# Loading the first group of rows in pieces of 6, 31 and 28 in place of 6, 28 and 31

## The chip, the core and the metric

The kernel runs on one core of a Trainium2 chip. The metric is the device time of one execution in microseconds. Three engines matter here: VectorE (DVE in the profile), which multiplies, ScalarE (ACT), which computes two sigmoids and a few rows, and SyncE (SP), which issues most DMAs. The 16 DMA engines of the core move the data; each of the two queues that are used here (q1, filled by SP, and q10, filled by ACT) is served in order, and the 16 engines share the packets of each transfer.

## What is computed

For 16,384 rows (tokens) of 512 float32 numbers, the two largest of 8 router logits are turned into two weights, and each row is written twice, once times each weight, the smaller first.

```python
    probs = probs / np.sum(probs, axis=-1, keepdims=True)
    topk_indices = np.argsort(probs, axis=-1)[..., -k:]
    topk_probs = np.take_along_axis(probs, topk_indices, axis=-1)
    topk_probs = topk_probs / np.sum(topk_probs, axis=-1, keepdims=True)
    x_expanded = x[:, :, np.newaxis, :].repeat(k, axis=2)
    return (x_expanded * topk_probs[..., np.newaxis]).astype(np.float32)
```

33.6 MB of rows and 0.5 MB of logits are read, 67.1 MB are written. With two weights left, the quotient of exponentials is a sigmoid of the difference of the two logits.

## The kernel before

Each of the 128 partitions holds 128 rows. They are worked in two groups, of 65 and 63 rows per partition (`GROUPS`); "a row" below means one row on each partition, 256 KB in all. `xs` holds the x rows of a group (65 rows of 2 KB per partition), `osp` has room for 18 output rows of 4 KB. `WA` holds the two weights of every row.

For a group, the loop over `LOADS[g]` (lines 121 to 146) issues the loads, each a run of consecutive rows. Behind the first load of group 1 (6 rows) SP issues the two loads of logits, which land in `osp`, and `top2_weights` (lines 15 to 38) computes all weights on VectorE and ScalarE. Then the loop over `STORES[g]` (lines 148 to 177) makes the outputs. Each entry is (first row, number of rows, place, position there): the multiply at line 164 writes the rows twice, times the weights, into `osp` or, for "xs", in place over rows of `xs` that are no longer needed, and line 176 issues the store, from ACT for the very first, from SP for all others. SP issues in the order of the program, and a DMA that has to wait holds up those behind it.

Group 1 has five stores: 3 rows through `osp` 0 to 2, 15 rows (3 to 17) through `osp` 3 to 17, 16 rows (18 to 33) in place, 15 rows (34 to 48) through `osp` 0 to 14, and 16 rows (49 to 64) in place. The fourth overwrites buffers of the first and the second. Its multiply is therefore cut in two (`FREE`, line 152): 3 rows (34 to 36), which need only the first store to have landed, and 12, which need the second. The order in which the instructions stand on VectorE is made by the scheduler of the language, the DMAs keep the order of the program.

Group 2 begins by loading over `xs`: a load of 4 rows from ACT, held back by a small operation (line 128) until the last store but one of group 1 has landed, then 28 and 31 rows from SP. Its four stores follow the same pattern, with a cut of 2 and 13 rows.

Of the kernel before, what the change touches and what calls it, by code (L numbers as in the profile page):

```python
# [1 line left out]

# [4 lines left out]

F32 = mybir.dt.float32
ALU = mybir.AluOpType
ACTF = mybir.ActivationFunctionType  # L10
P = 128


def top2_weights(nc, WA, dlt, room, logits, E):

    tt = nc.vector.tensor_tensor
    hi, lo, n = None, None, E  # L20
    while n > 1:
        n //= 2
        if hi is None:
            a, b = logits[:, :, 0:n], logits[:, :, n : 2 * n]
            nhi, nlo = room(n), b
            tt(nhi, a, b, op=ALU.max)  # L26
            tt(nlo, a, b, op=ALU.min)  # L27
        else:
            a, b = hi[:, :, 0:n], hi[:, :, n : 2 * n]
            nhi, nlo, tmp = room(n), room(n), room(n)  # L30
            tt(tmp, lo[:, :, 0:n], lo[:, :, n : 2 * n], op=ALU.max)  # L31
            tt(nlo, a, b, op=ALU.min)  # L32
            tt(nlo, nlo, tmp, op=ALU.max)  # L33
            tt(nhi, a, b, op=ALU.max)  # L34
        hi, lo = nhi, nlo
    tt(dlt, hi[:, :, 0], lo[:, :, 0], op=ALU.subtract)  # L36
    nc.scalar.activation(WA[:, :, 0], dlt, ACTF.Sigmoid, scale=-1.0)  # L37
    nc.scalar.activation(WA[:, :, 1], dlt, ACTF.Sigmoid, scale=1.0)  # L38

GROUPS = [65, 63]

LOADS = [[6, 28, 31], [4, 28, 31]]
BASE = [0, 1]

STORES = [
    [(0, 3, "osp", 0), (3, 15, "osp", 3), (18, 16, "xs", 0), (34, 15, "osp", 0), (49, 16, "xs", 33)],
    [(0, 16, "osp", 2), (16, 16, "xs", 0), (32, 15, "osp", 0), (47, 16, "xs", 32)],
]  # L50

L = 18

FREE = [3, 2]

ACT_ROWS = 2


@with_exitstack
def kernel(  # L60
    ctx: ExitStack,
    tc: tile.TileContext,
    x: bass.AP,
    router_logits: bass.AP,
    k: bass.AP,
    out: bass.AP,
):
    nc = tc.nc
    B, S, D = x.shape
    E = router_logits.shape[-1]  # L70
    N = B * S
    assert int(k) == 2 and E == 8 and N == P * sum(GROUPS)
    M = N // P

    x_v, o_v, rl_v = [], [], []
    t0 = 0
    for n in GROUPS:
        t1 = t0 + P * n
        x_v.append(
            x.rearrange("b s d -> (b s) d")[t0:t1].rearrange("(p m) d -> p m d", p=P)  # L80
        )
        o_v.append(
            out.rearrange("b s k d -> (b s) k d")[t0:t1].rearrange(
                "(p m) k d -> p m k d", p=P
            )
        )
        rl_v.append(
            router_logits.rearrange("b s e -> (b s) e")[t0:t1].rearrange(
                "(p m) e -> p m e", p=P
            )  # L90
        )
        t0 = t1

    wpool = ctx.enter_context(tc.tile_pool(name="wpool", bufs=1))
    xs = wpool.tile([P, max(GROUPS), D], F32)
    osp = wpool.tile([P, L, 2, D], F32)
    WA = wpool.tile([P, M, 2], F32)
    dlt = wpool.tile([P, M], F32)


    flat = osp.rearrange("p l k d -> p (l k d)")
    taken = [0]

    def room(n):
        o = taken[0]
        taken[0] += M * n
        return flat[:, o : o + M * n].rearrange("p (m n) -> p m n", n=n)

    logits = room(E)

    def place(where, at, n):

        if where == "osp":
            return osp[:, at : at + n]
        return xs[:, at : at + 2 * n, :].rearrange("p (r k) d -> p r k d", k=2)

    m0 = 0
    stores = []
    for g, G in enumerate(GROUPS):
        x0, r = BASE[g], 0  # L120
        for n in LOADS[g]:

            late = g == 1 and r == 0
            if late:


                rows = xs[:, x0 : x0 + 2, :]
                pause = nc.scalar.activation(rows, rows, ACTF.Copy)  # L128
                tc.add_manual_dep(
                    pause.ins,  # L130
                    stores[-2].ins.name,
                    mybir.DependencyInfo(
                        mybir.DependencyClass.Sync, mybir.DependencyReason.DATA
                    ),
                    reason="begin when the store ahead of the last has landed",
                )
                tc.keep_in_program_order(pause)
            queue = nc.scalar if late else nc.sync
            load = queue.dma_start(xs[:, x0 + r : x0 + r + n, :], x_v[g][:, r : r + n, :])  # L139
            tc.keep_in_program_order(load)  # L140
            r += n
            if g == 0 and r == 6:
                n0 = GROUPS[0]
                tc.keep_in_program_order(nc.sync.dma_start(logits[:, :n0], rl_v[0]))  # L144
                tc.keep_in_program_order(nc.sync.dma_start(logits[:, n0:], rl_v[1]))  # L145
                top2_weights(nc, WA, dlt, room, logits, E)
        assert r == G
        for r, n, where, at in STORES[g]:
            og = place(where, at, n)

            again = where == "osp" and at == 0 and r > 0
            cuts = [0, FREE[g], n] if again else [0, n]
            if g == 1 and r == 0:
                cuts = [0, n - ACT_ROWS]
                for j in range(n - ACT_ROWS, n):
                    for k2 in range(2):
                        nc.scalar.activation(  # L157
                            og[:, j, k2, :],
                            xs[:, x0 + r + j, :],
                            ACTF.Copy,  # L160
                            scale=WA[:, m0 + r + j, k2 : k2 + 1],
                        )
            for a, b in zip(cuts, cuts[1:]):
                nc.vector.tensor_tensor(  # L164
                    og[:, a:b],
                    xs[:, x0 + r + a : x0 + r + b, :]
                    .unsqueeze(2)
                    .to_broadcast([P, b - a, 2, D]),
                    WA[:, m0 + r + a : m0 + r + b, :]
                    .unsqueeze(3)  # L170
                    .to_broadcast([P, b - a, 2, D]),
                    op=ALU.mult,
                )

            queue = nc.scalar if g == r == 0 else nc.sync
            stores.append(queue.dma_start(o_v[g][:, r : r + n], og))  # L176
            tc.keep_in_program_order(stores[-1])
        m0 += G


# [1 line left out]
_INS = ['x', 'router_logits', 'k']  # L182
_OUTS = [((16, 1024, 2, 512), 'float32')]

_NUMBERS = {'k': 2}


# [26 lines left out]
```

## Time and profile before

| | us |
|---|---|
| three runs: median (lowest to highest) | 239.54 (239.52 to 239.55) |
| the profiled execution, its own time | 239.64 |
| its span, first to last instruction | 237.9 |
| VectorE busy | 139.8 |
| ScalarE busy | 5.4 |
| TensorE, GpSimd | nothing that counts |

Line numbers in the profile are those of the listing above. A row of the timeline has the start, the duration, the engine, the line, the operation, the tile written and the tile read, their shapes in elements per partition (1,024 of the output to a row: 3072 is three rows, 15360 fifteen, 16384 sixteen), and in brackets the idle time before it and what ended it. "SPq" and "ACTq" are DMA issues. A row of the windows has the stretch, its length, the busy time of VectorE, ScalarE and GpSimd with their instructions, the clock, the busy share of the DMA engines and GB/s; DMA packets count in the window in which they start. Rows of DMA issues give the KB of each and the us from issue to landing.

### The profile page before, as it was taken

What the parts mean: (1) busy time and instruction counts of PE and PEld (TensorE: products, weight loads), DVE (VectorE), ACT (ScalarE), POOL (GpSimd) and SP (SyncE); (2) the same over time, 40 slices, a digit from 0 to 9 for tenths busy, and PEclk for the clock granted to TensorE, in tenths of its full rate; (3) what the DMA queues carried; (4) which work ended last, traced back from release to release, by engine and by line L of the source; (5) the groups of instructions that cost most, each with busy time, mean ns of one, the idle gap of its engine ahead of it and who ended that gap; (6) DMA issues with size and microseconds to landing.
All of it is one profiled execution on the core that took longest, in us unless ns stands there. A gap on an engine that the chain in (4) does not pass through costs nothing.

```text
span 237.9 us, 111 instructions
## 1 busy us (share of the span) xinstructions
DVE 139.8 (59%) x22; ACT 5.4 (2%) x8; POOL 0.2 (0%) x4
## 2 busy tenths in 40 slices
DVE  0650499999689999200000009999976999950000
ACT  2000000000000000010000003000000000000000
POOL 0000000000000000000000000000000000000000
DMA  7989998989998989989998999898998989989894
GB/s 266 550 357 481 441 408 375 486 351 496 397 463 353 529 362 465 496 353 415 555 397 350 444 479 470 384 507 364 485 397 386 496 353 507 465 362 518 353 529 176
DMA packets 2448, 101.19 MB, mean 425 GB/s; under 512 B 272, under 2 KB 400, under 8 KB 528
## 3 DMA queue, kind: packets, MB, share of 16 engines
q1 hardware_dynamic: 2160, 98.57, 96.2%
q10 hardware_dynamic: 288, 2.62, 2.6%
HBM read 34.08 MB, written 67.11 MB: 425 GB/s over the span
## 4 chain that ended last, share of the span: by engine, by line
DMA 49%; DVE 39%; SPq 1%; issue 0%; DVEq 0%
DMA xs<-in_x_dram 29%; DVE osp L164 25%; DMA out_dram<-osp 19%; DVE xs L164 14%; SPq L144 0%; SPq L145 0%; SPq L139 0%; SPq L176 0%; DVEq L164 0%
## 5 line engine op out<-in xcount | busy, mean ns | idle before, releaser
L164 DVE TENSOR_TENSOR osp<-xs,WA 128x3072 f32<-128x3072 f32 (+5 forms) x7 | 67.2, 9604 | 63.5 <-DMA xs<-in_x_dram 56.9
L164 DVE TENSOR_TENSOR xs<-xs,WA 128x16384 f32<-128x16384 f32 x4 | 68.9, 17225 | 0.2
L26 DVE TENSOR_TENSOR osp<-osp 128x512 f32<-128x512 f32 x1 | 0.7, 691 | 8.1 <-DMA osp<-in_router_logits_dram 8.1
L157 ACT ACTIVATE osp<-xs,WA 128x512 f32<-128x512 f32 x4 | 2.6, 709 | 37.6 <-DMA xs<-in_x_dram 37.6
L128 ACT ACTIVATE xs<-xs 128x1024 f32<-128x1024 f32 x1 | 1.1, 1056 | 91.1 <-DMA out_dram<-osp 91.1
L37 ACT ACT_TABLE_LOAD x1 | 1.3, 1283 | 0.7 <-PEq L195 0.7
L27 DVE TENSOR_TENSOR osp<-osp 128x512 f32<-128x512 f32 x1 | 0.7, 691 | 0.0
L32 DVE TENSOR_TENSOR osp<-osp 128x256 f32<-128x256 f32 (+1 forms) x2 | 0.7, 352 | 0.0
L34 DVE TENSOR_TENSOR osp<-osp 128x256 f32<-128x256 f32 (+1 forms) x2 | 0.7, 351 | 0.0
L33 DVE TENSOR_TENSOR osp<-osp 128x256 f32<-128x256 f32 (+1 forms) x2 | 0.7, 351 | 0.0
L31 DVE TENSOR_TENSOR osp<-osp 128x256 f32<-128x256 f32 (+1 forms) x2 | 0.7, 350 | 0.0
L37 ACT ACTIVATE WA<-dlt 128x128 f32<-128x128 f32 x1 | 0.3, 315 | 10.0 <-DVE dlt L36 10.0
L36 DVE TENSOR_TENSOR dlt<-osp 128x128 f32<-128x128 f32 x1 | 0.3, 291 | 0.0
L38 ACT ACTIVATE WA<-dlt 128x128 f32<-128x128 f32 x1 | 0.3, 298 | 0.0
L195 POOL MEMSET const-uint8-127<- 128x1 uint8 x1 | 0.1, 102 | 0.0
L195 POOL MEMSET const-bfloat16-1.0<- 128x1 bf16 x1 | 0.1, 101 | 0.0
L195 POOL MEMSET const-float32-0.0<- 128x1 f32 x1 | 0.1, 98 | 0.2 <-issue 0.2
L195 POOL MEMSET const-float32-1.0<- 128x1 f32 x1 | 0.1, 98 | 0.0
## 6 DMA issues: line engine op xcount, KB each, us to landing
out_dram<-osp SPq DMA_DIRECT2D x3, 7680.0 KB, 23.3
xs<-in_x_dram SPq DMA_DIRECT2D x2, 7936.0 KB, 40.7
xs<-in_x_dram SPq DMA_DIRECT2D x2, 7168.0 KB, 35.1
xs<-in_x_dram SPq DMA_DIRECT2D x1, 1536.0 KB, 5.9
out_dram<-osp ACTq DMA_DIRECT2D x1, 1536.0 KB, 24.8
xs<-in_x_dram ACTq DMA_DIRECT2D x1, 1024.0 KB, 24.8
osp<-in_router_logits_dram SPq DMA_DIRECT2D x1, 260.0 KB, 6.2
osp<-in_router_logits_dram SPq DMA_DIRECT2D x1, 252.0 KB, 6.3
```

The costliest lines, as they stand in the source:

```text
L26: tt(nhi, a, b, op=ALU.max)
L27: tt(nlo, a, b, op=ALU.min)
L31: tt(tmp, lo[:, :, 0:n], lo[:, :, n : 2 * n], op=ALU.max)
L32: tt(nlo, a, b, op=ALU.min)
L33: tt(nlo, nlo, tmp, op=ALU.max)
L34: tt(nhi, a, b, op=ALU.max)
L36: tt(dlt, hi[:, :, 0], lo[:, :, 0], op=ALU.subtract)
L37: nc.scalar.activation(WA[:, :, 0], dlt, ACTF.Sigmoid, scale=-1.0)
L128: pause = nc.scalar.activation(rows, rows, ACTF.Copy)
L157: nc.scalar.activation(og[:, j, k2, :], xs[:, x0 + r + j, :], ACTF.Copy, scale=WA[:, m0 + r + j, k2 : k2 + 1],)
L164: nc.vector.tensor_tensor(og[:, a:b], xs[:, x0 + r + a : x0 + r + b, :] .unsqueeze(2) .to_broadcast([P, b - a, 2, D]), WA[:, m0 + r + a : ...
L195: nc = _bacc.Bacc("TRN2", target_bir_lowering=False, num_devices=1)
```

## The change

Only the sizes of the first group's second and third load are exchanged:

```diff
-LOADS = [[6, 28, 31], [4, 28, 31]]
+LOADS = [[6, 31, 28], [4, 28, 31]]
```

Rows 34 to 36, which came with the third load, now come with the second. The stores, their rows and their buffers are as they were. In the compiled kernel SP issues 128x15872 elements before 128x14336, and on VectorE one instruction stands elsewhere and the wait for the third load has gone to another (`-` before, `+` after; the elements are those per partition, the waits are those for DMAs):

```diff
 L164 TensorTensor osp<-xs,WA 128x15360    waits for: second load
+L164 TensorTensor osp<-xs,WA 128x3072    waits for: first store
 L164 TensorTensor xs<-xs,WA 128x16384
-L164 TensorTensor osp<-xs,WA 128x3072    waits for: third load, first store
-L164 TensorTensor osp<-xs,WA 128x12288    waits for: second store
+L164 TensorTensor osp<-xs,WA 128x12288    waits for: second store, third load
```

ScalarE, GpSimd and TensorE have the same instructions in the same order.

## The prediction

> **What bounds the kernel now.** I read the page first, then windows that cover the whole execution, then the timeline of the first group, and last, narrow windows at the places where one transfer follows another.
>
> ```profile
> span 237.9 us, 111 instructions
> ...
> DMA packets 2448, 101.19 MB, mean 425 GB/s; under 512 B 272, under 2 KB 400, under 8 KB 528
> ...
> DMA 49%; DVE 39%; SPq 1%; issue 0%; DVEq 0%
> ```
> ```profile
> 42.00:82.00 40.00, 37.29 (x5) 0.00 (x0) 0.00 (x0) 1.00 1.00 431
> 82.00:122.00 40.00, 14.37 (x1) 1.06 (x1) 0.00 (x0) 1.00 1.04 449
> 122.00:162.00 40.00, 19.56 (x2) 2.56 (x4) 0.00 (x0) 1.00 0.98 423
> 162.00:202.00 40.00, 36.59 (x4) 0.00 (x0) 0.00 (x0) 1.00 1.02 442
> 202.00:236.00 34.00, 9.62 (x1) 0.00 (x0) 0.00 (x0) 1.00 0.97 420
> ```
>
> In a windows row the last two columns are the mean busy share of the 16 DMA engines and GB/s; a packet is put down whole to the window in which it starts. From 42 to 236 us, in five equal steps but for the last, the share stays between 0.97 and 1.04: there is no stretch in which the DMA engines lack work, and 101.19 MB must pass through them. VectorE is on 39% of the chain of waits, but only because each of its waits ends with a transfer that is itself in a full queue. So the kernel is bound by the DMA engines, and a microsecond in which they idle is a microsecond of the end. The question for any edit here is not whether VectorE waits longer, but whether the DMA queue runs dry.
>
> ```profile
> 15.91 0.38 ACTq L176 DMA_DIRECT2D out_dram<-osp  x1
> 26.82 16.16 DVE L164 TENSOR_TENSOR osp<-xs,WA 128x15360 f32<-128x15360 f32 x1 [10.94 <-DMA xs<-in_x_dram]
> 43.00 0.35 SPq L176 DMA_DIRECT2D out_dram<-osp  x1
> 43.01 17.22 DVE L164 TENSOR_TENSOR xs<-xs,WA 128x16384 f32<-128x16384 f32 x1
> 60.15 3.35 DVE L164 TENSOR_TENSOR osp<-xs,WA 128x3072 f32<-128x3072 f32 x1
> 60.26 0.34 SPq L176 DMA_DIRECT2D out_dram<-xs  x1
> 66.15 12.96 DVE L164 TENSOR_TENSOR osp<-xs,WA 128x12288 f32<-128x12288 f32 x1 [2.64 <-DMA out_dram<-osp]
> 79.13 0.33 SPq L176 DMA_DIRECT2D out_dram<-osp  x1
> ```
>
> I number the stores of group 1 as the list STORES has them, 1 to 5. Store 2 (15 rows) is issued at 43.00, store 3 (16 rows, in place in `xs`) at 60.26, store 4 at 79.13. The three-row multiply at 60.15 prepares the beginning of store 4 and runs after the large multiply whose end lets store 3 go.
>
> ```profile
> 44.60:44.70 0.10, 0.10 (x1) 0.00 (x0) 0.00 (x0) 1.00 1.61 635
> 47.10:47.15 0.05, 0.05 (x1) 0.00 (x0) 0.00 (x0) 1.00 2.85 1229
> 65.20:65.25 0.05, 0.00 (x0) 0.00 (x0) 0.00 (x0) 1.00 0.00 0
> 65.25:65.30 0.05, 0.00 (x0) 0.00 (x0) 0.00 (x0) 1.00 6.07 2622
> 65.70:65.80 0.10, 0.00 (x0) 0.00 (x0) 0.00 (x0) 1.00 1.52 655
> 65.80:67.60 1.80, 1.45 (x1) 0.00 (x0) 0.00 (x0) 1.00 0.00 0
> ```
>
> The last packets of the third load begin from 44.6 us on, the first packets of store 2 at 47.1, those of store 3 between 65.25 and 65.8. Store 2's 7.86 MB (15 rows of 4 KB on 128 partitions) from 47.1 to 65.25 is 433 GB/s, full rate. So store 2 waited 4.1 us in the queue before its first packet, and store 3 five (65.25 - 60.26). These two leads are the reserve that the change spends.
>
> **The change, part by part.** Bytes, instructions and DMAs keep their number: 6, 31 and 28 rows are issued in place of 6, 28 and 31, on the same queue, and no wait is new in kind. Two things move.
>
> First, the second load is 3 rows longer. They are 3 x 128 x 2048 B = 0.786 MB, at the rate of 434 GB/s that the next row shows 1.81 us.
>
> ```profile
> DMA packets 256, 13.01 MB, mean 434 GB/s; under 512 B 48, under 2 KB 48, under 8 KB 48
> ```
> ```profile
> 15.60:16.20 0.60, 0.28 (x1) 0.00 (x0) 0.00 (x0) 1.00 3.53 1529
> 17.70:18.30 0.60, 0.00 (x0) 0.00 (x0) 0.00 (x0) 1.00 3.78 1529
> 23.05:23.60 0.55, 0.00 (x0) 0.00 (x0) 0.00 (x0) 1.00 3.99 1460
> 25.50:26.50 1.00, 0.00 (x0) 0.00 (x0) 0.00 (x0) 1.00 1.08 457
> ```
>
> (The 434 GB/s are the stretch from 40 to 70 us.) Packets of the second load start 2.1 us apart, one per engine. Its last ones start at 23.05 to 23.6 and the next packets, small ones of store 1, from 25.5 on: about 0.4 us more than 2.1. If that excess does not come again, the load lands only 1.4 us later; if one more of store 1's packets (12,288 B at 434/16 = 27.1 GB/s, 0.45 us) slips in ahead of its end, 2.3 later. I take 1.8, the bytes alone: the 15-row multiply begins at 28.63 (28.2 to 29.1) and ends 16.16 later, and store 2 is issued at 44.81 in place of 43.00. The third load ends when it did, at 47.1 to 47.65, since the bytes of all loads together are the same. So store 2 still has 2.3 us of lead; its nearest relation is the first store of group 2:
>
> ```profile
> 157.51 0.34 SPq L176 DMA_DIRECT2D out_dram<-osp  x1
> ```
> ```profile
> 158.40:160.00 1.60, 1.60 (x1) 0.00 (x0) 0.00 (x0) 1.00 0.00 0
> 160.00:160.10 0.10, 0.10 (x1) 0.00 (x0) 0.00 (x0) 1.00 1.52 655
> ```
>
> It was issued 2.5 us ahead of its first packet and the load before it was at full rate to the end. I cost this part at nothing; the cover is the last packets of the third load, and where it fails by 0.2 to 0.3 us the loss isn't added to what follows, since the lanes would then be busy that much longer with store 2.
>
> Second, rows 34 to 36, which the three-row multiply reads, now come with the second load and not with the third. In the order of the compiled kernel that multiply has moved ahead of the 16-row one on VectorE. It no longer waits for the third load (the 12-row multiply does, which runs long after that has landed); it still waits for store 1, whose buffer it overwrites. That store landed at 40.7:
>
> ```profile
> out_dram<-osp ACTq DMA_DIRECT2D x1, 1536.0 KB, 24.8
> ```
>
> 15.91 + 24.8. Even 2 us later this is before 44.8, so the wait costs nothing. But the 3.35 us of the multiply now stand ahead of the 16-row one and of store 3, which was not so before:
>
> - 28.63 + 16.16 + 3.35 - 0.08 (neighbours overlap: 43.01 + 17.22 is 60.23, the next began at 60.15) + 17.22 = 65.3, and store 3 is issued some 0.03 later, at 65.33 (64.9 to 65.8).
>
> That is 5.1 us later than 60.26, and the reserve was 5.0. SP has nothing else queued between stores 2 and 3, and ACT's queue is empty, so when store 2's last packets end at 65.25 to 65.8 the engines have nothing. What is lost is the time from the issue of a DMA into an empty queue to its running at full rate. No store of before shows this; the first load does:
>
> ```profile
> 0.73 0.37 SPq L139 DMA_DIRECT2D xs<-in_x_dram  x1
> xs<-in_x_dram SPq DMA_DIRECT2D x1, 1536.0 KB, 5.9
> ```
> ```profile
> 1.60:1.70 0.10, 0.00 (x0) 0.10 (x1) 0.00 (x0) 1.00 0.00 0
> 1.70:1.80 0.10, 0.00 (x0) 0.10 (x1) 0.00 (x0) 1.00 2.93 737
> ```
>
> First packet 1.0 us after the issue. Of its 5.9 us to landing, 1.57 MB take 3.6 at 434 GB/s and the end about 0.4 (the engines turned from store 2 to store 3 by 65.75, and VectorE was released by store 2's landing at 66.15). That leaves 1.9 us for start and filling. From above, the store at 157.51 bounds it at 2.5, as no gap was seen there. Between 1.0 and 2.5 I take 1.5, the middle of the two readings of the first load, which is the only DMA on an empty queue.
>
> - Sum: 65.33 + 1.5 - 65.5 (the middle of the starts of store 3 before) = +1.3 us. Bounds: 64.9 + 1.0 - 65.5 = +0.4 and 65.8 + 2.5 - 65.5 = +2.8.
>
> The Trainium skill ("DMA: Bandwidth & Descriptors", section "Latency and other measured facts") gives about 600 ns to the first byte for DMAs issued as these are; by that the sum would be +0.4. The same page ("Anatomy of one DMA") has about 2.0 us of fixed cost per DMA, most of it the receipt at the end; by that, +1.8. The first load's 1.0 lies above the one figure, and its 1.9 by the other.
>
> Where the delay goes: store 4's multiply needs store 2 landed (66.15) and VectorE free (65.3), so it begins at 66.15 as before, and store 4 is still issued at 79.13, now with 1.3 us more reserve. Everything behind store 3 in the queue moves by 1.3 us, and the loads of group 2 with it. There each stage waits for a landing and none for the clock, and the windows above show no idle stretch that could absorb it. So it reaches the end whole.
>
> The profiled execution took 239.64 us (span 237.9 and 1.7 around it), 0.10 above the median of 239.54. 239.64 + 1.3 = 240.9; from the median 240.85, which I forecast.
>
> **Rivals.**
>
> *No loss, or a small gain.* The last packets of the third load took from 44.6 to 47.1, about 2.5 us, where 63,488 B at 27.1 GB/s are 2.34. In group 2, where the store is issued only as the last load packets begin, no such excess is seen:
>
> ```profile
> 157.70:157.75 0.05, 0.05 (x1) 0.00 (x0) 0.00 (x0) 1.00 2.93 1270
> ```
>
> 157.72 to 160.08 is 2.36. If an early store in the queue slows the last load packets, the change removes 0.15 us: 239.4. For it to show, store 3's issue would have to be covered: the three-row multiply would have to stay behind the 16-row one. Then store 3 goes at 28.63 + 16.16 + 17.22 = 62.0, over 3 us ahead of need, and 239.4 to 239.5 stands. Against it speaks the compiled order. It would also do if a store on an empty queue began within 0.2 us, and the first load's 1.0 speaks against that. Chance 0.09 for no difference, 0.03 for a gain above 0.5 us, which I can derive from no row.
>
> *A larger loss at the same place.* Start-up costs the full 2.5 us and load 2 lands at 29.1: +2.8, 242.3. It decides once the first packet of store 3 begins after 68. Chance 0.08. Only the overlap of the store at 157.51 leaves it open.
>
> *Store 2 is the one that starves.* If 2.3 us of lead are too few, there is a gap at 47.4 too. With 2.5 needed it is 0.2; store 2 then frees the engines 0.2 later and store 3's gap shrinks by as much. The end stays at 240.85; above 2.5 the group 2 row excludes it. So it has no time of its own, only another place, chance 0.05 and counted with the forecast.
>
> **How the numbers follow.** The main case (store 3 starves the queue, +0.4 to +2.0) has 0.80 and the larger loss 0.08; no change 0.09, gain 0.03. A measurement of this kernel tells about 0.2%, 0.5 us, from no change; of the main case the lowest corner, +0.4, falls under that, some 0.03. So faster 0.03, within 0.2% 0.12, slower 0.85. The range of 240.0 to 241.9 goes from +0.5 to +2.4: it leaves out the gain, most of no change and the top of the larger loss, under 2 in 10.
>
> **What would show it.** Right: in the changed profile the 15-row multiply begins near 28.6, a 3.35 us multiply stands between it and the 16-row one, store 3 is issued near 65.3, windows between 65.8 and 66.3 have packets still missing that should have started, and store 4 is still issued near 79.1, while the first large multiply of group 2, in the row below, begins 1.3 later. Wrong: packets of store 3 that begin by 65.8 as before; a gap at 47 instead; a three-row multiply that waits beyond 44.8; or a shift at 66 that is gone by 142.
>
> ```profile
> 142.35 15.09 DVE L164 TENSOR_TENSOR osp<-xs,WA 128x14336 f32<-128x14336 f32 x1 [45.98 <-DMA xs<-in_x_dram]
> ```

## The result and the profile after

| | median us | lowest to highest | runs |
|---|---|---|---|
| before | 239.55 | 239.52 to 239.67 | 5 |
| changed | 241.65 | 241.54 to 241.78 | 5 |

The ratio is 1.0087, with a 95% interval of 1.0072 to 1.0102: 2.1 us slower, on the forecast side and inside the range, 0.8 us above the forecast time. The profiled execution took 241.65.

The page and the windows of the changed kernel:

```profile
span 239.9 us, 112 instructions
...
DMA packets 2448, 101.19 MB, mean 422 GB/s; under 512 B 272, under 2 KB 400, under 8 KB 528
```
```profile
42.00:82.00 40.00, 39.17 (x5) 0.00 (x0) 0.00 (x0) 1.00 0.98 426
82.00:122.00 40.00, 14.33 (x1) 1.06 (x1) 0.00 (x0) 1.00 0.98 419
122.00:162.00 40.00, 17.83 (x2) 2.56 (x4) 0.00 (x0) 1.00 1.00 426
```

The same packets and bytes as before, in a span 2.0 us longer. Two microseconds are lost in 240, so a window of 40 us shows them only in its last digits, and an edge that takes in one packet more or less (0.97 to 1.04 before) moves as much. The timeline places them:

```profile
44.94 0.35 SPq L176 DMA_DIRECT2D out_dram<-osp  x1
48.09 17.22 DVE L164 TENSOR_TENSOR xs<-xs,WA 128x16384 f32<-128x16384 f32 x1
65.34 0.34 SPq L176 DMA_DIRECT2D out_dram<-xs  x1
66.11 12.96 DVE L164 TENSOR_TENSOR osp<-xs,WA 128x12288 f32<-128x12288 f32 x1 [0.80 <-DMA out_dram<-osp]
79.09 0.33 SPq L176 DMA_DIRECT2D out_dram<-osp  x1
...
105.48 0.34 ACTq L139 DMA_DIRECT2D xs<-in_x_dram  x1
...
144.08 15.09 DVE L164 TENSOR_TENSOR osp<-xs,WA 128x14336 f32<-128x14336 f32 x1 [47.75 <-DMA xs<-in_x_dram]
...
182.28 14.03 DVE L164 TENSOR_TENSOR osp<-xs,WA 128x13312 f32<-128x13312 f32 x1 [3.60 <-DMA out_dram<-osp]
```

and, for the two of these that were not shown of before:

```profile
104.70 0.34 ACTq L139 DMA_DIRECT2D xs<-in_x_dram  x1
...
180.33 14.03 DVE L164 TENSOR_TENSOR osp<-xs,WA 128x13312 f32<-128x13312 f32 x1 [3.37 <-DMA out_dram<-osp]
```

Each of these rows hangs on a landing, so its shift is what the DMA queue has lost by then: 0 at 66 (66.11 against 66.15), 0.78 at 105, 1.73 at 144, 1.95 at 182. The loss has four places. Windows of the changed kernel at each of them (packets count where they start):

```profile
65.34:66.10 0.76, 0.00 (x0) 0.00 (x0) 0.00 (x0) 1.00 0.01 0
66.10:66.20 0.10, 0.09 (x1) 0.00 (x0) 0.00 (x0) 1.00 7.67 3277
66.20:66.35 0.15, 0.15 (x1) 0.00 (x0) 0.00 (x0) 1.00 11.25 4806
108.60:108.85 0.25, 0.00 (x0) 0.00 (x0) 0.00 (x0) 1.00 10.79 4194
122.45:122.70 0.25, 0.00 (x0) 0.00 (x0) 0.00 (x0) 1.00 11.56 4194
159.40:159.95 0.55, 0.55 (x1) 0.00 (x0) 0.00 (x0) 1.00 4.86 1847
```

and of the kernel before at the last three:

```profile
107.50:108.05 0.55, 0.00 (x0) 0.00 (x0) 0.00 (x0) 1.00 4.40 1907
...
121.00:121.65 0.65, 0.00 (x0) 0.00 (x0) 0.00 (x0) 1.00 4.02 1739
...
157.70:158.30 0.60, 0.60 (x1) 0.00 (x0) 0.00 (x0) 1.00 3.90 1693
```

First, store 3 is issued at 65.34 and no data packet starts for 0.76 us; then five start by 66.20 and the other eleven by 66.35 (3277 GB/s over 0.10 us and 4806 over 0.15, in packets of 65,536 bytes). That is the gap.

The other three are no gaps: the next transfers were long in the queue. The packets took longer. As a packet counts whole where it starts, share times length is the mean time of an engine's packets that start there, and each of the three windows holds one packet per engine.

| window | where | mean time of a packet, changed | before |
|---|---|---|---|
| 108.60 | packets of store 5 just ahead of the first ones of the four-row load | 2.70 | 2.42 |
| 122.45 | turn from store 5 to group 2's loads | 2.89 | 2.42 |
| 159.40 | turn from group 2's loads to its first store | 2.67 | 2.34 |

(The row of before at 121 also holds ten packets of 8 KB of the four-row load, 0.19 us of its 2.61.) That is 0.28, 0.47 and 0.33 us. With the 0.76 of the gap the means add up to 1.84 of the 1.95; a transfer has landed only when its slowest engine is done, so means can fall short.

### The profile page after: what moved, and what is told of

It reads as the page before. It is cut to its first block, busy times and chain, and to the rows that moved or that the text cites. A ratio compares the mean times of both kernels' runs of the same rounds, so it can differ in the third digit from the quotient of the medians.

```text
span 239.9 us, 112 instructions
## 1 busy us (share of the span) xinstructions
DVE 139.7 (58%) x22; ACT 5.4 (2%) x8; POOL 0.2 (0%) x4
## 4 chain that ended last, share of the span: by engine, by line
DMA 49%; DVE 39%; SPq 1%; issue 0%; DVEq 0%
DMA xs<-in_x_dram 31%; DVE osp L164 24%; DMA out_dram<-osp 18%; DVE xs L164 14%; SPq L144 0%; SPq L145 0%; SPq L139 0%; SPq L176 0%; DVEq L164 0%
```

## The experiments

Times are medians, each beside the kernel before on the same chip in the same session (239.60 to 239.70). Single executions of the kernel before reach 240.83 and 240.98 in two of these sessions, so one high time in a run is not a loss of that run.

### Is the gap the whole cause?

Theory 1 was that the emptied queue causes the 0.75 us and the slow packets behind it too. Run 1 puts the three-row multiply back behind the 16-row one:

```diff
+                made = nc.vector.tensor_tensor(
...
+                if g == 0 and r > 3:
+                    tc.keep_in_program_order(made)
```

> Loads of 6, 31 and 28 rows as in the changed kernel, but the three-row multiply stands behind the 16-row one again, as before the change. Theory 1 (the gap ahead of store 3 is the cause of the whole 2.1 us: 0.75 us directly and some 1.2 us in slower packets behind it): store 3 is issued near 62.0, its first packets begin at 65.2 to 65.4 with no gap, no slow packets in group 2, and the time is 239.3 to 239.6. Rival (the late store 2, or the sizes of the loads, are what slow the later packets): no gap at 65 either, but the packets near 109, 122 and 159 us are still slow, and the time is 240.4 to 240.8.

241.73 (241.46 to 241.98), 2.06 above before. The gap is gone, the loss isn't:

```profile
62.24 0.34 SPq L178 DMA_DIRECT2D out_dram<-xs  x1
```
```profile
65.20:65.38 0.18, 0.18 (x1) 0.00 (x0) 0.00 (x0) 1.00 5.93 2563
65.38:65.90 0.52, 0.10 (x1) 0.00 (x0) 0.00 (x0) 1.00 2.62 1132
...
124.46:124.80 0.34, 0.00 (x0) 0.00 (x0) 0.00 (x0) 1.00 2.33 795
...
160.10:160.80 0.70, 0.70 (x1) 0.00 (x0) 0.00 (x0) 1.00 2.38 1030
160.80:162.10 1.30, 1.30 (x1) 0.00 (x0) 0.00 (x0) 1.00 0.00 0
162.10:162.50 0.40, 0.40 (x1) 0.00 (x0) 0.00 (x0) 1.00 0.76 328
162.50:162.90 0.40, 0.40 (x1) 0.00 (x0) 0.00 (x0) 1.00 4.16 1802
```

Store 3's 16 first packets (7 + 9 of 65,536 B) start between 65.2 and 65.9 as before. At 160 the first packets of group 2's first store should start on 16 engines within 0.6 us, as they did before; 1030 GB/s over 0.70 us are 11 packets, two more start between 162.1 and 162.5, and the last three only after that. So theory 1 falls in this form: without any gap, five engines still come some 2 us late out of group 2's loads. The multiply that waits for this store to land begins at 182.47, 2.14 us later than before, as late as the late engines. They begin to fall behind at the turn to group 2's loads: from 124.46 to 124.80 four packets of 57,344 bytes start, 2.12 us each, and five of 8 KB from the four-row load, which leaves 0.84 us for each of these five where such a packet takes 0.31. The rival named the direction, but its 240.4 to 240.8 was 0.9 us and more too low.

Run 2 removes the cut of the 15 rows altogether:

```diff
-            again = where == "osp" and at == 0 and r > 0
+            again = g == 1 and where == "osp" and at == 0 and r > 0
```

> Loads of 6, 31 and 28 rows, and the 15 rows of store 4 are multiplied in one piece (group 1 is not cut), so that nothing can stand ahead of the 16-row multiply. Store 3 is issued near 62.0 again; store 4 near 66.1 + 16.2 = 82.3 in place of 79.1, where store 3 keeps the queue busy until 84.6. Theory 1: no gap, 239.3 to 239.6. Rival (late store 2 or load sizes): 240.4 to 240.8.

241.41 (241.18 to 242.26), 1.74 above before, store 3 again at 62.18 without a gap. The rival's direction holds again, its 240.4 to 240.8 doesn't: the new place of the three-row multiply is not needed for the loss.

Run 3 makes the gap alone, with the loads of before and the multiplies of group 1 in the program's order. The added multiplies write into `osp` rows that are written again later:

```diff
+            if g == 0 and r == 18:
+                for n0, k1 in ((3, 2), (3, 1)):
+                    o = osp[:, 0:n0, 0:k1]
+                    i = xs[:, 6 : 6 + n0, :].unsqueeze(2).to_broadcast([P, n0, k1, D])
+                    w = WA[:, 6 : 6 + n0, 0:k1].unsqueeze(3).to_broadcast([P, n0, k1, D])
+                    tc.keep_in_program_order(nc.vector.tensor_tensor(o, i, w, op=ALU.mult))
```

> The loads of before (6, 28, 31), with two extra multiplies of three rows and three half rows (5.0 us of VectorE, into buffers that are written again later) ahead of the 16-row multiply. Store 2 is issued at 43.0 as before, store 3 near 65.3 in place of 60.26. Theory 1: a gap of 0.7 to 0.8 us ahead of store 3 and slow packets in group 2 as in the changed kernel, 241.3 to 241.8 in all. Rival (late store 2 or load sizes slow the later packets): the gap alone, 240.2 to 240.4.

241.82 (241.67 to 241.94), 2.15 above before: here theory 1 holds, at the top of its forecast and to the pattern.

```profile
65.45:66.15 0.70, 0.70 (x1) 0.00 (x0) 0.00 (x0) 1.00 0.00 0
66.15:66.40 0.25, 0.25 (x1) 0.00 (x0) 0.00 (x0) 1.00 7.37 3146
122.40:122.75 0.35, 0.00 (x0) 0.00 (x0) 0.00 (x0) 1.00 6.87 2458
122.75:125.20 2.45, 0.00 (x0) 0.00 (x0) 0.00 (x0) 1.00 0.28 107
```

With the old sizes, a gap of the same length brings the same slow turn at 122. So each of two things, a gap ahead of store 3 or the new loads without a gap, costs 2.1 us, and in the changed kernel, which has both, they cost 2.1 us together. Its trace looks like run 3's, not like run 1's: after the gap all 16 engines begin store 3 within 0.25 us and are all slow at the turn at 122, where run 1 has a few engines out of step.

Run 4 puts the added multiplies of run 3, now both of three whole rows, into the kernel with the changed loads; the real three-row multiply stands behind the 16-row one. Against run 3, beside `LOADS`:

```diff
-                for n0, k1 in ((3, 2), (3, 1)):
+                for n0, k1 in ((3, 2), (3, 2)):
```

> Loads of 6, 31 and 28 rows, with two extra multiplies of three rows (6.7 us of VectorE) ahead of the 16-row one and the real three-row multiply behind it: store 3 is issued near 68.7, 3.35 us later than in the changed kernel. Theory 1 with a price per emptied queue that doesn't grow with the length of the gap: 241.65 + 3.35 = 245.0. If the slow packets grow with the gap: 246 or more. If the queue had still covered a part at 65.3: under 244.5.

245.18 (245.09 to 245.20), 5.51 above before, so 3.41 more than the 2.10 of the changed kernel. Store 3 went at 68.94, 3.60 us later than in the changed kernel. The wait at store 3 passes nearly whole to the end, and the part that comes later doesn't grow with the length of the gap.

### What in the new loads costs without a gap?

Either the sizes, or store 2's issue, which moved from 43.00 to 44.94, where the last load packets of group 1 begin. Theory 2 was the late store. Run 5 delays store 2 with the loads of before and the multiplies of group 1 in the program's order:

```diff
+            if g == 0 and r == 3:
+                o = osp[:, 3:6, 0:1]
+                i = xs[:, 6:9, :].unsqueeze(2).to_broadcast([P, 3, 1, D])
+                w = WA[:, 6:9, 0:1].unsqueeze(3).to_broadcast([P, 3, 1, D])
+                tc.keep_in_program_order(nc.vector.tensor_tensor(o, i, w, op=ALU.mult))
```

> The loads of before (6, 28, 31), with 1.8 us of extra VectorE work (three half rows) ahead of the 15-row multiply: store 2 is issued near 44.8 in place of 43.0, as the last packets of the third load begin, store 3 near 62.0, so that nothing starves. Theory 2 (a store that is issued only as the last load packets begin leaves the engines without the next packets read ahead, and they pay at the next turn between stores and loads): the last load packets of group 1 take 2.34 us in place of 2.5, some packets of store 5 near 107 to 124 and of group 2's loads are slow, and the time is 241.3 to 242.0. Rival (the sizes 31 and 28 do it): 239.5 to 239.8.

240.96, but spread from 239.49 to 242.28 over ten runs, where before stayed within 239.50 to 240.01. Store 2 went at 44.79, store 3 at 62.05, so there was no gap. Four of the ten runs lie at the rival's 239.5 to 239.8, four in theory 2's 241.3 to 242.0, one between them (240.59) and one above both (242.28). The sizes were those of before, so in six of ten runs a late store 2 alone brings a loss.

Run 6 takes the new sizes and gets store 2 out early, with two of its rows on ScalarE and the order of run 1:

```diff
-            if g == 1 and r == 0:
+            if (g == 1 and r == 0) or (g == 0 and r == 3):
                 cuts = [0, n - ACT_ROWS]
```

> Loads of 6, 31 and 28 rows, the three-row multiply behind the 16-row one, and two of store 2's 15 rows multiplied by ScalarE (2.85 us beside VectorE), so that store 2 is issued near 28.75 + 14.05 = 42.8, before the last load packets begin, and store 3 near 60.0. Theory 2: the last load packets of group 1 are slow (2.5 us in place of 2.12 + 0), nothing is slow in group 2, 239.3 to 239.7. Rival (the sizes 31 and 28 do it): 241.4 to 241.9.

239.61 (one of ten runs at 240.74, the others 239.57 to 239.83), 0.01 above before, ratio 0.9995 to 1.0015. The sizes 31 and 28 cost nothing once store 2 is early.

Run 7 is the same edit in the kernel before.

> The kernel before with two of store 2's rows multiplied by ScalarE: store 2 is issued near 26.8 + 14.05 = 40.9 in place of 43.0, everything else as before. Theory 2: 239.4 to 239.7, nothing slow in group 2. A third possibility, that the kernel before is free of slow packets in group 2 only by the chance of its phases and any shift of store 2 brings them: 241 to 242.

239.62 (one at 240.82), ratio 0.9996 to 1.0016. The kernel before is not a lucky point: store 2 can go 2 us earlier and nothing changes.

Run 8 goes between, with one row on ScalarE in place of run 6's two:

```diff
-                cuts = [0, n - ACT_ROWS]
-                for j in range(n - ACT_ROWS, n):
+                act = ACT_ROWS if g == 1 else 1
+                cuts = [0, n - act]
+                for j in range(n - act, n):
```

> As the run with two of store 2's rows on ScalarE and the three-row multiply behind the 16-row one, but with one row on ScalarE: store 2 is issued near 28.7 + 15.1 = 43.8, 1.2 us ahead of the last load packets of group 1 (near 45.0), store 3 near 61.0. Between the 1.9 us of lead that cost nothing and the 0.3 us that cost 2.1. If store 2 has only to be issued ahead of the last packets by the 0.8 us that a store needs to its first packet: 239.5 to 239.8. If it takes a whole packet (2.1 us) or nearly so: 241 to 242, or runs between.

240.97, spread from 239.53 to 241.59 over ten runs. Store 2 went at 44.03; in the profile the last load packets begin between 45.0 and 45.6.

| run | store 2 issued | middle of the last load packets' starts | lead | time above before |
|---|---|---|---|---|
| 7 | 40.97 | 44.85 | 3.9 | 0.02 |
| 6 | 42.80 | 45.15 | 2.3 | 0.01 |
| before | 43.00 | 44.85 | 1.8 | 0 |
| 8 | 44.03 | 45.15 | 1.1 | 1.27, spread over 2 us |
| 2 | 44.92 | 45.1 | 0.2 | 1.74, spread over 1.1 us |
| 1 | 44.98 | 45.2 | 0.2 | 2.06 |
| 5 | 44.79 | 44.85 | 0.1 | 1.36, spread over 2.8 us |

The starts are read from windows of 0.1 us. At a lead of 1.8 us and more the median shows no loss (single executions of runs 6 and 7 reach 240.74 and 240.82, as single ones of before do); at 1.1 and less there is one, of 0 to 2.7 us, and it varies from one execution to the next. It doesn't fall in order (run 5 is less hurt than run 1), so the lead is not all that decides below 1.8.

Theory 2 had named a sign: where store 2 is late, the last load packets are no longer slow. It came. First run 7, then run 8, at these packets:

```profile
44.70:45.30 0.60, 0.60 (x1) 0.00 (x0) 0.00 (x0) 1.00 4.14 1693
```
```profile
44.50:45.30 0.80, 0.80 (x1) 0.00 (x0) 0.00 (x0) 1.00 2.48 1075
```

In run 7 the 16 packets of 63,488 bytes took 2.48 us in the mean, 0.14 more than the 2.34 that they need. In run 8 the 15 packets of 57,344 bytes in the window took 2.12, just what they need.

### Where is it paid, and is it avoidable?

Run 9 takes the changed kernel and issues group 2's four-row load from SP, so that no second queue is mixed into store 5; run 10 is the control with the kernel before.

```diff
-            queue = nc.scalar if late else nc.sync
+            queue = nc.sync
```

> The changed kernel, with the four-row load of group 2 issued from SP's queue in place of ScalarE's: it then stands behind store 5 in one queue and no engine serves stores and loads in turn. The gap of 0.75 us ahead of store 3 stays. If the 1.2 us that were lost behind the gap come from the two queues being mixed at that turn: 240.2 to 240.6. If they come with any turn from stores to loads: 241.3 to 241.9.

> The kernel before with the same other queue for the four-row load, as the control: 239.4 to 239.8 if the queue by itself costs nothing; what it differs from 239.6 is taken off the run with the changed loads.

241.72 (241.59 to 241.88) and 239.69 (239.60 to 239.80): the queue costs nothing, and the loss stays. First run 9, then run 10, at the last packets of store 5:

```profile
120.50:120.80 0.30, 0.00 (x0) 0.00 (x0) 0.00 (x0) 1.00 4.93 1529
120.80:123.60 2.80, 0.00 (x0) 0.00 (x0) 0.00 (x0) 1.00 0.60 211
123.60:124.20 0.60, 0.00 (x0) 0.00 (x0) 0.00 (x0) 1.00 0.72 287
```
```profile
119.30:119.90 0.60, 0.00 (x0) 0.00 (x0) 0.00 (x0) 1.00 3.27 1420
119.90:121.70 1.80, 0.00 (x0) 0.00 (x0) 0.00 (x0) 1.00 0.25 109
```

In run 9 the last packet of store 5 took 3.16 us per engine in the mean (4.93 x 0.30 + 0.60 x 2.80), in run 10 2.41 (3.27 x 0.60 + 0.25 x 1.80). Between the issue of the four-row load (105.44 against 104.66) and group 2's first large multiply (144.18 against 142.38) run 9 loses 1.02 us, and some 0.75 of it sit in this one packet at the turn from stores to loads. So behind a gap the loss belongs to the turn, not to the mixing. For the kernels without a gap no run tests this: the five late engines of run 1 fall behind at the same turn, but there it could still come from the two queues.

Run 11 is the changed kernel with its own order and two of store 2's rows on ScalarE (run 6 without the kept order):

```diff
-            if g == 1 and r == 0:
+            if (g == 1 and r == 0) or (g == 0 and r == 3):
```

> The changed kernel with its own order (the three-row multiply ahead of the 16-row one) and two of store 2's rows multiplied by ScalarE: store 2 is issued near 42.8, store 3 near 28.7 + 14.03 + 3.3 + 17.22 = 63.2, 2 us ahead of need. If what costs is the emptied queue or a late store 2, and neither the order nor the sizes by themselves: 239.5 to 239.8. If the order by itself costs: 240.5 or more.

239.63 (239.61 to 239.86), ratio 0.9969 to 1.0019.

```profile
42.79 0.35 SPq L176 DMA_DIRECT2D out_dram<-osp  x1
45.88 17.22 DVE L164 TENSOR_TENSOR xs<-xs,WA 128x16384 f32<-128x16384 f32 x1
63.13 0.34 SPq L176 DMA_DIRECT2D out_dram<-xs  x1
```

Loads of 31 and 28 and the three-row multiply ahead, yet the whole 2.1 us are gone: both stores are issued 2 us and more ahead of need again, and nothing else of the change was taken back.

Run 12 issues store 1 from SP, behind the loads, to save the slow packets of the second load:

```diff
-            queue = nc.scalar if g == r == 0 else nc.sync
+            queue = nc.sync
```

> The kernel before with its first store issued from SP's queue, behind the loads: the loads of group 1 are no longer mixed with a store, so the 0.15 and 0.40 us by which the sixth and last packets of the second load were too long should go, and store 2 is issued near 41. If these are a cost of mixing: 238.9 to 239.2, faster than both kernels. If they only move to the turn from loads to stores: 239.4 to 239.7.

240.23 (240.12 to 240.29), ratio 0.9991 to 1.0041, though its four runs all lie 0.48 us or more above before's median of 239.64. Neither forecast holds. The slow packets of the second load went (the 15-row multiply began at 25.03 in place of 26.82), and the turn to store 1 became slow in their place:

```profile
40.70:41.40 0.70, 0.67 (x2) 0.00 (x0) 0.00 (x0) 1.00 3.32 998
41.40:44.10 2.70, 2.70 (x1) 0.00 (x0) 0.00 (x0) 1.00 0.05 23
44.10:44.80 0.70, 0.70 (x1) 0.00 (x0) 0.00 (x0) 1.00 0.95 404
```

3.4 us from the last load packets to the next, where 63,488 B at 27.1 GB/s need 2.34: 1.1 us at one turn. Store 1 was issued at 16.03, over 24 us ahead of these load packets, so a long lead alone does not make a turn free. No version here beats the kernel before; runs 6, 7, 10 and 11 equal it.

## Why the prediction was right, and where it was not

**The bound.** Right: a microsecond without work for the DMA engines was a microsecond of the end, as run 4 shows.

**The second load and store 2's issue.** The 15-row multiply was forecast for 28.63 and store 2 for 44.81; store 2 went at 44.94. Right in time.

**Store 3's issue.** Forecast 65.33, measured 65.34, with the three-row multiply ahead of the 16-row one. Store 4 was forecast unchanged at 79.13 and went at 79.09. Right.

**The start of an empty queue.** The term was mis-sized: 1.5 us was taken, the middle of two readings of the first load; it was 0.9 (from 65.34 to about 66.25, the middle of the 16 starts), a little under the lower reading of 1.0. What the gap moves is therefore about 0.75 (66.25 less 65.5) and not 1.3. The Trainium skill's 600 ns to the first byte ("DMA: Bandwidth & Descriptors", "Latency and other measured facts") was nearer than the value chosen, and some 0.2 us short of the first packets, which begin between 66.10 and 66.20. The 2.0 us of fixed cost that the prediction took from the same page of the Trainium skill ("Anatomy of one DMA") are given there for DMAs that GpSimd issues and lie mostly at the end of a transfer; they are no price of a start, and no run here shows them.

**"Everything behind store 3 in the queue moves by 1.3 us."** This step failed. The shift grew from 0.78 at 105 to 1.73 at 144 and 1.95 at 182. The sign that the prediction named, group 2's first large multiply 1.3 later, came out at 1.73. After the gap, packets are slower by 0.28 us where the four-row load comes in, and by 0.47 and 0.33 at the next two turns between stores and loads. The forecast assumed a queue that is full again to be as good as one that was never empty; run 3 shows that it isn't. The two errors have opposite signs, 0.55 us too much at the start and 1.35 too little behind it, so that the forecast missed by only 0.8: that 241.65 lies in a range that ends at 241.9 is in part luck.

**Store 2's later issue costed at nothing.** No gap came at 47, as forecast, but the step failed all the same: run 1 has the late store 2 without the gap and loses 2.06 us, and run 6, with the same sizes and an early store 2, loses nothing. The first store of group 2, which was taken as the nearest relation, went 0.5 us ahead of its last load packets without harm; but no turn to loads follows it, and the harm is seen at such a turn.

**The rivals.** "No loss" was to follow if the three-row multiply stayed behind. Run 1 did just that and gave 241.73 in place of 239.4, so this rival had a wrong price. Its gain of 0.15 us, from last load packets that an early store no longer slows, is in the trace only up to the next turn. The larger loss of 2.8 from a slower start did not come; store 2 was not starved.

**What stays open.** That a gap costs its length and about 1.3 us more is shown (run 3), and that store 2, issued 1.8 us or more ahead of the last load packets, costs nothing. Why isn't. A reading that fits is that each engine fetches the next packet while it moves the present one, and has to build this lead up again when it was lost: run 12 then pays 1.1 us at the first turn, the kernel before in the slow packets of its second load, and kernels with a gap pay again. One thing in the trace of before speaks for it. ACT issues the four-row load at 104.70; with a start of 0.9 us its packets could follow those of store 5 that end from 107.5 on, but every engine takes one more packet of store 5 first, and the load's begin only from 109.9 on:

```profile
107.50:108.05 0.55, 0.00 (x0) 0.00 (x0) 0.00 (x0) 1.00 4.40 1907
109.90:109.95 0.05, 0.00 (x0) 0.00 (x0) 0.00 (x0) 1.00 0.39 164
```

The first row is 16 packets of store 5, the second one packet of 8 KB of the load (0.31 us). No run measures the fetching itself. Nor is it known why the loss varies in runs 5 and 8 and hardly in run 1, or why the loss isn't the sum of two causes in the changed kernel.

## What to carry to other kernels

In a kernel bound by its DMA engines, write down for every transfer how long before its first packet it was issued; a change that shifts work ahead of the issue is free only while that lead stays above what the start of a transfer takes (0.9 us here for an empty queue), and with a margin: for store 2, at a turn from loads to stores, 1.8 us was enough and 1.1 was not. A gap can cost more than its length, and the rest shows up 40 to 100 us later, most of it at the next turns, so follow the shift of several landings through the whole timeline before taking the first one for the sum. After changing the size of a load, look at the compiled order of the instructions too: rows that arrive earlier can let the scheduler move a multiply ahead of the one that a store waits for.

## What was not expected of the hardware

Packets of one size took the same time for most of the run (2.42 us for 65,536 bytes at 107.5 in the kernel before), and most exceptions stand where the second queue comes in and at turns: 0.28 us at 108.6 and 0.47 at the turn from stores to loads after a gap, 1.1 at the turn in run 12. The DMA engines can also fall out of step: in run 1 five of 16 left group 2's loads about 2 us behind the others, no gap having gone before, and nothing later brought them together.
